# One queue for all transfers, or the stores of the weight sums on GpSimd's own

## The chip, the cores and the metric

The kernel runs on one core of a Trainium2 chip. A core has TensorE (PE in the profile), VectorE (DVE), ScalarE (ACT), GpSimd (POOL) and SyncE (SP), each with its own queue of instructions that run in order. The metric is the time of one execution in microseconds (us).

## The reference, cut to what matters

Two layers of a trunk over 1024 rows of width 1024. Layer 0 mixes with a gated MLP, layer 1 with differential attention; after each comes a ConvFFN. The large products are those of the ConvFFN, 1024 -> 5632 and 2816 -> 1024:

```python
def conv_ffn(x, w_up, conv_w, conv_b, w_down):
    h = causal_dwconv(x @ w_up, conv_w, conv_b)
    g, u = h[..., :D_FF], h[..., D_FF:]
    return (jax.nn.gelu(g) * u) @ w_down
```

with `D_FF = 2816`, and for layer 1 the product `y @ w_in` that makes the values of the attention.

## The kernel before, in words

All products run in float32 split into two fp32r parts: `split` (L168) lets ScalarE cast the high part (L170) and VectorE subtract the low part (L173), and every product is three passes of matmuls (`mm`, L160, the matmul at L162).

The products are Winograd products: a product of 2 by 2 blocks takes seven block products in place of eight, and for that needs sums of weight blocks. There are two kinds of them.

- **Up-projection weights.** `ffn` (L1142) works through 22 pairs `j` of columns. For each pair `winograd_weights` (L1029) loads two raw tiles `wr` from `in_ffn_up` by `raw_w` (L177, 512 KB each), and GpSimd makes four sums from them: L1044, L1047, L1048, L1052, always in that order on its queue. ScalarE and VectorE split the blocks and the sums (`w<-wr`, `w<-wt`) into a ring of seven `w4` tiles, which TensorE uses. ScalarE's cast of L1052's sum is its third `w<-wt` cast of a pair. The two L1153 per pair are the start of the convolution, once TensorE has made the pair's columns.
- **Down-projection and value weights.** These sums are needed only later, so `weight_sum` (L429) makes them early, one small piece at a time, and puts them aside in DRAM: it loads a piece of `in_ffn_down` (or `in_b_wv`) into a `wr` tile by two transfers (L438), lets GpSimd do four subtractions in place on 128x256 (L442 to L445), and stores the tile's two halves to `td` (or `tv`) by two transfers (L447, 256 KB each). Pairs 4 to 21 of both layers make one such sum each, pairs 8, 11, 14 and 17 two; pairs 2 and 3 of layer 0 make one for `tv`, and six more for `tv` are made in the gated MLP of layer 0. That is 52 sums and 104 stores.

The `wr` tiles of both kinds come from one ring of four buffers. In the built program the first `in_ffn_up` load of pair j+1 takes the very buffer that the sum of pair j was stored from. In a pair with two sums the second sum's load takes that buffer, and after its store the second load of pair j+1.

All transfers are begun by SP's one queue, in the order of the built program, which a scheduler fixes. A transfer that waits holds up the ones behind it.

In the gated MLP (`gmlp`), GpSimd also adds the spatial gate (L645), ScalarE copies the next gate out of PSUM (L643) into one of two buffers that L645 reads, and behind that copy on ScalarE's queue stand casts (L170) for TensorE.

Of the kernel before, what the change touches and what calls it, by code (L numbers as in the profile page):

```python
# [64 lines left out]
def trunk(ctx: ExitStack, tc: tile.TileContext, io):  # L65
    nc = tc.nc
# [7 lines left out]
    def nm(s):  # L74
        uid[0] += 1
        return f"{s}_{uid[0]}"
# [352 lines left out]
    def weight_sum(w, o, j):  # L429

        a = wpool.tile([P, 2, 2, 256], F32, tag="wr", name=nm("wr"), bufs=4)
        kt, cs = j // 2, slice(j % 2 * 256, j % 2 * 256 + 256)
        for k in range(2):
            src = w[kt + k * o.shape[1]].rearrange("p (b c) -> p b c", b=2)
            nc.sync.dma_start(a[:, k], src[:, :, cs])  # L438

        def rest():  # L440
            sub = nc.gpsimd.tensor_tensor
            sub(a[:, 0, 0], a[:, 0, 1], a[:, 0, 0], ALU.subtract)  # L442
            sub(a[:, 0, 1], a[:, 1, 1], a[:, 0, 1], ALU.subtract)
            sub(a[:, 1, 1], a[:, 1, 1], a[:, 0, 0], ALU.subtract)
            sub(a[:, 1, 0], a[:, 1, 0], a[:, 1, 1], ALU.subtract)  # L445
            for k in range(2):
                nc.sync.dma_start(o[k, kt][:, :, cs], a[:, k])  # L447

        return rest

# [892 lines left out]
```

## Time and profile before

| | us |
|---|---|
| median of 3 runs | 2171.81 (2171.61 to 2175.49) |
| the profiled execution | 2170.53 |
| its span | 2168.8 |
| TensorE busy in the span | 2113.0 (97%) |
| VectorE busy | 1660.5 (77%) |
| ScalarE busy | 1094.4 (50%) |
| GpSimd busy | 748.1 (34%) |

The profile is one execution. Its span is the time from the first to the last instruction; the profiled execution took 1.7 us more. Instructions that begin transfers do not count as busy; in a timeline they stand as SPq. The FFN of layer 0 lies at about 308 to 740 us, that of layer 1 at about 1510 to 1950 us, the gated MLP before 215 us.

### The profile page before, as it was taken

To read this page: it belongs to the slowest core of one execution; us is meant where nothing else is said; L and a number is where in the kernel's file an instruction comes from. 1 tells how busy PE (TensorE), PEld (TensorE's weight loads), DVE (VectorE), ACT (ScalarE), POOL (GpSimd) and SP (SyncE) were. 2 spreads that over 40 slices of the span, in tenths; PEclk is the share of its full clock that TensorE was granted. 3 is DMA by queue.
4 is the path that set the end of the run, shared out by engine and by line. 5 is a ranking of instruction groups with operands and counts; after the bars stand their busy time and mean duration, and the time that the engine had idled before them with its cause. 6 is when DMAs were issued, how large, how long until landed. Compare 5 with 4: busy or idle time off the path is not lost.

```text
span 2168.8 us, 27265 instructions
## 1 busy us (share of the span) xinstructions
PE 2113.0 (97%) x10008; PEld 1721.4 (79%) x10008; DVE 1660.5 (77%) x2031; ACT 1094.4 (50%) x1923; POOL 748.1 (34%) x691
## 2 busy tenths in 40 slices
PE   8989998999999999999999999999899999999998
PEld 7868776888888878887777777778688888888886
DVE  5755569878888786688588888866988888888756
ACT  7423435454545544465366665754555554454533
POOL 0463136666667000042001101222555666620012
PEclk9999999999999999999999999999999999999999
DMA  8332422544444562453411110233234444457324
GB/s 320 102 122 83 176 87 82 192 149 153 146 165 146 198 251 95 136 180 106 158 45 45 50 49 21 88 136 126 70 121 167 159 156 157 154 182 266 105 92 167
DMA packets 159270, 292.82 MB, mean 135 GB/s; under 512 B 12704, under 2 KB 77088, under 8 KB 159136
## 3 DMA queue, kind: packets, MB, share of 16 engines
q1 hardware_dynamic: 159136, 291.08, 39.3%
q8 instruction: 78, 1.28, 0.2%
q14 instruction: 56, 0.46, 0.1%
HBM read 214.49 MB, written 76.55 MB: 134 GB/s over the span
## 4 chain that ended last, share of the span: by engine, by line
PE 74%; DVE 9%; ACT 3%; issue 1%; POOL 0%; DMA 0%; DVEq 0%; ACTq 0%; POOLq 0%; SPq 0%
PE ps L162 70%; PE pst L162 2%; DVE t L173 2%; DVE w L173 1%; ACT e L885 1%; DVE t L1155 1%; PE pst L904 1%; PE pst L334 1%; DVE cols L1090 1%; DVE xs L344 0%; DVE e L891 0%; DVE h L385 0%; DVE sm L882 0%; DVE t L495 0%; ACT y L340 0%
## 5 line engine op out<-in xcount | busy, mean ns | idle before, releaser
L162 PE MATMUL ps<-t,w 128*128 128x512 f32 x4848 | 1150.8, 394 | 19.5 <-ACT tm L1086 7.8
L162 PEld LDWEIGHTS ps<-t,w 128*128 128x128 f32 x4848 | 899.2, 188 | 220.8 <-ACT tm L1086 11.6
L162 PE MATMUL ps<-w,t 128*128 128x512 f32 x2512 | 590.5, 392 | 9.0 <-ACT w L170 7.3
L162 PEld LDWEIGHTS ps<-w,t 128*128 128x128 f32 x2512 | 469.4, 188 | 107.1 <-ACT w L170 8.0
L173 DVE TENSOR_TENSOR w<-wr,w 128x512 fp32r<-128x512 f32 (+1 forms) x274 | 290.4, 1066 | 170.0 <-ACT w L170 84.3
L170 ACT CAST w<-wr 128x512 fp32r<-128x512 f32 (+1 forms) x276 | 219.1, 802 | 207.3 <-PE ps L162 195.2
L1155 DVE SCALAR_TENSOR_TENSOR t<-cols,cw,t 128x1023 f32<-128x1023 f32 (+1 forms) x176 | 264.1, 1500 | 18.9 <-ACT t L1153 16.8
L173 DVE TENSOR_TENSOR w<-wt,w 128x512 fp32r<-128x512 f32 x176 | 174.9, 1005 | 15.4 <-ACT w L170 15.2
L1086 ACT COPY tm<-ps 128x512 f32<-128x512 f32 x136 | 78.9, 580 | 146.7 <-PE ps L162 146.6
L173 DVE TENSOR_TENSOR t<-t,t 128x1024 fp32r<-128x1024 f32 (+1 forms) x124 | 134.0, 1109 | 14.4 <-ACT t L170 14.0
L170 ACT CAST t<-t 128x1024 fp32r<-128x1024 f32 (+1 forms) x124 | 105.7, 889 | 71.7 <-PE ps L162 59.4
L1153 ACT ACTIVATE t<-cols,cw 128x1024 f32<-128x1024 f32 x88 | 109.7, 1247 | 60.0 <-DVE cols L1090 59.8
L1044 POOL TENSOR_TENSOR wt<-wr,wr 128x512 f32<-128x512 f32 x44 | 67.3, 1529 | 195.5 <-DMA wr<-in_ffn_up 135.4
L162 PE MATMUL ps<-t,t 64*128 64x512 f32 (+4 forms) x792 | 128.3, 373 | 0.8 <-ACT e L885 0.4
L170 ACT CAST w<-wt 128x512 fp32r<-128x512 f32 x176 | 107.5, 622 | 23.2 <-PE ps L162 14.1
L559 POOL TENSOR_TENSOR v<-v,u 128x512 f32<-128x512 f32 x8 | 12.0, 1499 | 307.0 <-DVE u L558 307.0
L162 PEld LDWEIGHTS ps<-t,t 64*128 64x128 f32 (+1 forms) x792 | 90.3, 185 | 34.3 <-issue 11.0
L885 ACT ACTIVATE e<-ps,sm 128x128 f32<-128x128 f32 (+7 forms) x128 | 94.2, 744 | 28.8 <-DVE sm L877 22.7
L380 POOL TENSOR_SCALAR sm<-sm 128x1 f32<-128x1 f32 x32 | 22.3, 697 | 244.9 <-ACT y L378 244.6
L202 POOL TENSOR_SCALAR sm<-sm 128x1 f32<-128x1 f32 (+1 forms) x42 | 12.7, 303 | 263.7 <-ACT ot L924 161.2
L1090 DVE TENSOR_TENSOR cols<-ps,tm 128x512 f32<-128x512 f32 x132 | 90.1, 682 | 16.7 <-PE ps L162 15.0
L173 POOL TENSOR_TENSOR t<-wr,t 128x1024 fp32r<-128x1024 f32 (+1 forms) x16 | 36.4, 2282 | 167.9 <-ACT t L170 159.7
(156 smaller groups left out, 2480.4 us busy)
## 6 DMA issues: line engine op xcount, KB each, us to landing
wr<-in_ffn_up SPq DMA_DIRECT2D x88, 512.0 KB, 4.0
wr<-in_ffn_down SPq DMA_DIRECT2D x94, 256.0 KB, 3.7
pd<-t SPq DMA_DIRECT2D x88, 256.0 KB, 2.6
td<-wr SPq DMA_DIRECT2D x88, 256.0 KB, 2.5
wr<-td SPq DMA_DIRECT2D x40, 512.0 KB, 3.7
t<-pd SPq DMA_DIRECT2D x16, 1024.0 KB, 8.2
wr<-in_ffn_down SPq DMA_DIRECT2D x30, 512.0 KB, 3.6
hd<-h SPq DMA_DIRECT2D x24, 512.0 KB, 2.6
```

The costliest lines, as they stand in the source:

```text
L162: nc.tensor.matmul(o, a, b, start=first, stop=last, skip_group_check=onto)
L170: i = nc.scalar.copy(hi, src)
L173: return (engine or nc.vector).tensor_tensor(lo, src, hi.bitcast(F32), ALU.subtract)
L334: nc.tensor.transpose(pt[:, k * P:(k + 1) * P], xs[:, f:f + P], ident)
L380: nc.gpsimd.tensor_scalar(ss, sq[:, 0:1], sq[:, 1:2], EPS, ALU.add, ALU.add)
L885: nc.scalar.activation(e[:, :L], si[i], AF.Exp, bias=negm[:, i:i + 1], accum_out=sm[:, i:i + 1])
L904: nc.tensor.transpose(pt[:, k * P:(k + 1) * P], attn[:, c:c + P], ident)
L1044: i = nc.gpsimd.tensor_tensor(t1, b12, b11, ALU.subtract)
L1086: nc.scalar.copy(t, o)
L1090: nc.vector.tensor_tensor(o, a, b, ALU.add)
L1153: nc.scalar.activation(tt, src, AF.Identity, bias=c[:, 3:4], scale=c[:, 2:3])
L1155: nc.vector.scalar_tensor_tensor(tt[:, tap:], src[:, :S - tap], c[:, 2 - tap:3 - tap], tt[:, tap:], ALU.mult, ALU.add)
```

## The change

The two stores at the end of `weight_sum` are begun by GpSimd's queue. Nothing is computed differently.

```diff
             sub(a[:, 1, 1], a[:, 1, 1], a[:, 0, 0], ALU.subtract)
             sub(a[:, 1, 0], a[:, 1, 0], a[:, 1, 1], ALU.subtract)
             for k in range(2):
-                nc.sync.dma_start(o[k, kt][:, :, cs], a[:, k])
+                nc.gpsimd.dma_start(o[k, kt][:, :, cs], a[:, k])
```

The scheduler then orders the queues anew. The orders of TensorE, VectorE and ScalarE stay as they were. GpSimd's queue in pair 8 of layer 0, which makes two sums (`wr_3888` is the first sum's tile, `wr_3786` and `wr_3788` are the pair's raw weights, `wt_...` their sums):

```order
 L443 TENSOR_TENSOR wr_3888<-wr_3888 128x256
 L444 TENSOR_TENSOR wr_3888<-wr_3888 128x256
+L447 DMA td_77<-wr_3888 256x1x256
+L1048 TENSOR_TENSOR wt_3868<-wr_3786,wt_3866 128x512
 L445 TENSOR_TENSOR wr_3888<-wr_3888 128x256
-L1048 TENSOR_TENSOR wt_3868<-wr_3786,wt_3866 128x512
+L447 DMA td_77<-wr_3888 256x1x256
 L1052 TENSOR_TENSOR wt_3867<-wr_3788 128x512
```

The first store now stands on GpSimd's queue behind L444, L1048 has moved ahead of the last subtraction L445, and the second store stands behind that; this is so in pairs 5 to 21 of both layers, while in pairs 2 to 4 L1048 stays where it was relative to L445.

SP's queue in the same pair (`wr_3897` is the second sum's tile, `wr_3948` and `wr_3950` are the raw weights of pair 9):

```order
 L438 DMA wr_3888<-in_ffn_down 128x2x256 x2
-L447 DMA td_77<-wr_3888 256x1x256
 L1162 DMA pd_75<-t_3547 128x512 x2
-L447 DMA td_77<-wr_3888 256x1x256
 L438 DMA wr_3897<-in_ffn_down 128x2x256 x2
 L177 DMA wr_3948<-in_ffn_up 128x1024
-L447 DMA td_77<-wr_3897 256x1x256 x2
 L177 DMA wr_3950<-in_ffn_up 128x1024
```

The stores are gone and the loads keep their order; which buffer follows which in the ring is unchanged, so the loads that take a stored sum's buffer still wait for its stores to land.

GpSimd's queue in the gated MLP, at the third of the six `tv` sums (`wr_1551`; `wr_1632` is the fourth):

```order
 L444 TENSOR_TENSOR wr_1551<-wr_1551 128x256
+L447 DMA tv<-wr_1551 256x1x256
 L445 TENSOR_TENSOR wr_1551<-wr_1551 128x256
+L447 DMA tv<-wr_1551 256x1x256
 L645 TENSOR_TENSOR t_35_190<-t_35_190,gt_1065 128x256
+L645 TENSOR_TENSOR t_35_190<-t_35_190,gt_1074 128x256
+L645 TENSOR_TENSOR t_35_190<-t_35_190,gt_1083 128x256
 L442 TENSOR_TENSOR wr_1632<-wr_1632 128x256
-L645 TENSOR_TENSOR t_35_190<-t_35_190,gt_1074 128x256
```

Two stores come ahead of the gate additions L645, and two of these additions have moved ahead of the next sum's first subtraction.

## Rows read from the trace of the kernel before

**Rows 1.** Page, parts 1 and 3: busy us by engine; the data queue.

```profile
PE 2113.0 (97%) x10008; PEld 1721.4 (79%) x10008; DVE 1660.5 (77%) x2031; ACT 1094.4 (50%) x1923; POOL 748.1 (34%) x691
...
q1 hardware_dynamic: 159136, 291.08, 39.3%
```

**Rows 2.** Stretches of gated MLP and FFN 0: length, busy us by engine.

```profile
88.00:250.00 162.00, 151.93 (x692) 124.47 (x690) 91.10 (x127) 55.43 (x89) 69.27 (x126) 0.97 0.38 125
...
330.00:740.00 410.00, 403.79 (x1772) 331.78 (x1773) 348.40 (x337) 213.75 (x313) 250.36 (x178) 1.00 0.45 153
```

**Rows 3.** Timeline, pair 16 of layer 0: start us, length, instruction, idle before.

```profile
607.10 1.29 POOL L1044 TENSOR_TENSOR wt<-wr,wr 128x512 f32<-128x512 f32 x1 [3.46 <-DVE w L173]
...
613.29 0.74 POOL L445 TENSOR_TENSOR wr<-wr 128x256 f32<-128x256 f32 x1
...
615.58 0.57 SPq L447 DMA_DIRECT2D td<-wr  x1
...
618.55 0.81 SPq L177 DMA_DIRECT2D wr<-in_ffn_up  x2
...
623.49 1.60 POOL L1044 TENSOR_TENSOR wt<-wr,wr 128x512 f32<-128x512 f32 x1 [5.49 <-DMA wr<-in_ffn_up]
```

**Rows 4.** Timeline, pair 17 with two sums, then L1044 of pairs 18 and 20.

```profile
631.24 0.57 SPq L447 DMA_DIRECT2D td<-wr  x1
...
633.85 1.25 SPq L438 DMA_DIRECT2D wr<-in_ffn_down  x2
...
640.31 3.38 SPq L447 DMA_DIRECT2D td<-wr  x2
...
645.92 0.34 SPq L177 DMA_DIRECT2D wr<-in_ffn_up  x1
...
649.60 1.28 POOL L1044 TENSOR_TENSOR wt<-wr,wr 128x512 f32<-128x512 f32 x1 [6.50 <-DMA wr<-in_ffn_up]
...
681.63 1.34 POOL L1044 TENSOR_TENSOR wt<-wr,wr 128x512 f32<-128x512 f32 x1 [4.61 <-DMA wr<-in_ffn_up]
```

**Rows 5.** Waits of SP's queue: waiter, what released it: us, times, longest.

```profile
SPq L177 <- DMA td<-wr: 73.5, 36, 3.7
```

**Rows 6.** Timeline: L1153 of two pairs that follow each other, TensorE's pace.

```profile
652.03 1.25 ACT L1153 ACTIVATE t<-cols,cw 128x1024 f32<-128x1024 f32 x1
...
671.07 1.25 ACT L1153 ACTIVATE t<-cols,cw 128x1024 f32<-128x1024 f32 x1
```

**Rows 7.** GpSimd by shape, then VectorE: count, busy us, mean ns, idle before.

```profile
L1048 POOL TENSOR_TENSOR wt<-wr,wt 128x512 f32<-128x512 f32 x44 | 72.3, 1644 | 7.5 <-DVE w L173 7.3
...
L445 POOL TENSOR_TENSOR wr<-wr 128x256 f32<-128x256 f32 x52 | 60.0, 1155 | 3.8
...
L173 DVE TENSOR_TENSOR w<-wr,w 128x512 fp32r<-128x512 f32 (+1 forms) x274 | 290.4, 1066 | 170.0 <-ACT w L170 84.3
```

**Rows 8.** The stores: ns min/median/max to begin one; KB, us to landing.

```profile
L447 SPq DMA_DIRECT2D td<-wr x88: 560/562/569, 388.7 to 1913.1; - x88
...
td<-wr SPq DMA_DIRECT2D x88, 256.0 KB, 2.5
```

**Rows 9.** Timeline, pair 18: L1052, its cast, ScalarE's next copy.

```profile
659.10 2.28 POOL L1052 TENSOR_TENSOR wt<-wr 128x512 f32<-128x512 f32 x1
...
662.39 0.62 ACT L170 CAST w<-wt 128x512 fp32r<-128x512 f32 x1
...
664.63 0.59 ACT L1086 COPY tm<-ps 128x512 f32<-128x512 f32 x1 [1.61 <-PE ps L162]
```

**Rows 10.** Timeline, pair 21 of layer 0, then of layer 1: L1052, its cast.

```profile
707.31 1.74 POOL L1052 TENSOR_TENSOR wt<-wr 128x512 f32<-128x512 f32 x1
...
719.51 0.62 ACT L170 CAST w<-wt 128x512 fp32r<-128x512 f32 x1
...
1914.33 1.73 POOL L1052 TENSOR_TENSOR wt<-wr 128x512 f32<-128x512 f32 x1
...
1927.07 0.62 ACT L170 CAST w<-wt 128x512 fp32r<-128x512 f32 x1
```

**Rows 11.** Timeline, layer 1: L1044 of pair 3 and of pair 8.

```profile
1561.86 2.12 POOL L1044 TENSOR_TENSOR wt<-wr,wr 128x512 f32<-128x512 f32 x1 [4.38 <-DMA wr<-in_ffn_up]
...
1652.56 1.89 POOL L1044 TENSOR_TENSOR wt<-wr,wr 128x512 f32<-128x512 f32 x1 [4.39 <-DMA wr<-in_ffn_up]
```

**Rows 12.** Timeline, gated MLP: GpSimd, ScalarE and TensorE around one wait.

```profile
132.33 0.72 POOL L645 TENSOR_TENSOR t<-t,gt 128x256 f32<-128x256 f32 x1
...
133.08 0.37 ACT L643 COPY gt<-ps 128x256 f32<-128x256 f32 x1 [2.39 <-POOL t L645]
...
134.45 0.38 PE L162 MATMUL ps<-wsp,vp 128*128 128x256 f32 x1 [2.05 <-ACT vp L170]
```

## The prediction

> **What bounds the kernel now.** I read the busy shares first: TensorE is busy 2113.0 us of the span of 2168.8 [rows 1], so 55.8 us in all could be won, and any loss must come from a wait that is hidden today. The stretches come next. TensorE idles 10.1 us of 162 in the gated MLP, and 6.2 of 410 in FFN 0 [rows 2], where 88 of the 104 moved stores lie (both FFNs) and 4 more.
>
> So the question is what TensorE's work in the FFN hides. The timeline of GpSimd and SP shows a **loop** from one pair to the next [rows 3]: L1044 starts at 607.10, the sum's last store is begun at 615.58, the next raw weights' load goes out at 618.55, and the next L1044, released by that load, starts at 623.49. That is 8.5 + 3.0 + 4.9 = 16.4 us. The load waits for the store because it takes the buffer that the store reads; SP's queue stood so 36 times before an `in_ffn_up` load, 73.5 us in all [rows 5]. In a pair with two sums the loop has two stores in a row: from 623.49 over the stores at 631.24 and 640.31 and the loads at 633.85 and 645.92 to 649.60, 26.1 us [rows 3, 4]. TensorE's pace is 19.0 us a pair, from L1153 to L1153 [rows 6]. Three pairs, one of them with two sums, take the loop 681.63 - 623.49 = 58.1 us and TensorE 57.1. The loop has hardly any room on average: GpSimd lives on a lead over TensorE.
>
> How large that lead is, is read at L1052 and the ScalarE cast that takes its sum. In pair 18, after two sums, L1052 ends at 661.38 and the cast starts at 662.39, only 1.0 us later [rows 9]. In pair 21, the last, the gap is 719.51 - 709.05 = 10.5 us in layer 0 and 1927.07 - 1916.06 = 11.0 in layer 1 [rows 10]: this is what the loop may lose over a whole FFN before ScalarE waits.
>
> **The change part by part.** Removed: 104 stores from SP's queue, 0.56 us each to begin [rows 8]. SP is off TensorE's path except through the loop, where only the last store's 0.56 us counts; I take it off there and cost the other at nothing, since SP is then waiting for the landing anyway.
>
> Added: 104 stores on GpSimd's queue. No transfer of the profile is begun by GpSimd; all data go by one queue [rows 1], so their **price c** has to be bounded. Below, c = 0: GpSimd's sequencer hands it on and the engine goes on. Above, c = 2.5 us: GpSimd stands as long as such a store takes on SP from its start to its landing [rows 8]. The nearest rows are SP's 0.56 us for the very same transfer and GpSimd's own work on the very same data, one subtraction of 128x256 at 1.16 us [rows 7, 8]. I take 1.16, since it is an instruction of this engine over this tile and pays what this engine pays beside VectorE. For the landing after that I keep SP's 2.5 - 0.56 = 1.94 us.
>
> By the Trainium skill (DMA: Bandwidth & Descriptors, Specifications) the first byte comes after about 1 us on GpSimd's path and 0.6 on SP's; an estimate with c = 1.0 from that page would make the result about 2242. No run here shows it.
>
> Moved: L1048 goes ahead of the last subtraction in pairs 5 to 21, 1.64 us [rows 7], and so into the loop. Its sum comes no later, so that is all it does.
>
> The loop grows, for each pair: one sum, L1048 moved: 1.64 + 2c - 0.56 = 3.40. Two sums: 1.64 + 4c - 2 x 0.56 = 5.16. One sum, L1048 not moved (pair 4 of both layers, pairs 2 and 3 of layer 0): 2c - 0.56 = 1.76. The loop of pair 21 leads nowhere. Layer 0: 12 x 3.40 + 4 x 5.16 + 3 x 1.76 = 66.7 us. Layer 1: 12 x 3.40 + 4 x 5.16 + 1.76 = 63.2 us.
>
> What hides it: in layer 0 the 10.5 us, less 2c = 2.3, because two stores now stand ahead of L1052 too, plus what ScalarE can be late before TensorE stands. For the last term the ends are 1.6 us, ScalarE's idle time before its next copy out of PSUM [rows 9], and 9.1, its idle time in a pair (48% of 19.0, as 213.75 of 410 are busy [rows 2]); I take 5. That makes 13.2. In layer 1 it is 11.0 - 2.3 + 5 = 13.7, and 10.7 more: from pair 3 to pair 8 the loops took 90.7 us [rows 11], though five of 16.0 (the mean of pairs 18 and 19 [rows 4]) are 80.0; they waited there for buffers that TensorE's pace frees, and can take that back. That makes 24.4. When that cover is gone, TensorE runs at the loop's pace. So TensorE waits 66.7 - 13.2 = 53.5 us in layer 0 and 63.2 - 24.4 = 38.8 in layer 1, together 92.3.
>
> What gives some back: VectorE is busy 348.40 of 410 us [rows 2], and beside it a subtraction takes 1.16 us on average and can take 0.74, a sum of 512 columns 1.64 and 1.29 [rows 3, 7]. Four of the former and three of the latter in the loop lose 4 x 0.42 + 3 x 0.35 = 2.7 us to it. If the stretch grows by 46 us, VectorE's share falls from 85 to 76%, so 11% of that, 0.3 us, comes back in each of 36 loops: -11.
>
> The gated MLP: 12 stores, 13.9 us of GpSimd in a stretch where TensorE waits through ScalarE's copies for the additions L645 [rows 12]. At the wait shown two stores now stand ahead of it: up to +2.3. But two later additions now come ahead of a subtraction that waits for its load, and SP is free for that load. Ends: -10.1, all of TensorE's idle time there, and +13.9, all twelve on the path; I take +3, close to the one place that the rows show.
>
> Sum: 92.3 - 11 + 3 = +84 us. On the profiled execution that is 2170.5 + 84 = 2255; its median stands 1.3 higher, so 2256.
>
> **The rivals.**
> *Cheap stores.* For a price c the loops grow by 13.4 + 46c in layer 0 and 14.5 + 42c in layer 1, against a cover of 15.5 - 2c and 26.7 - 2c. Up to c = 0.04 both are hidden, whatever SP's queue does, and the time stays 2172; at c = 0.13 layer 0 is 4 us over (0.2%), at SP's 0.56 the sum is +34 and gives 2206. The same holds if the stores were not really carried out by GpSimd. For it: the small instructions of GpSimd are short. Against it: GpSimd's queue runs in order, and its rows of this size are not below 0.7 us. 0.11, of which 0.08 within 0.2%.
>
> *Dearer stores.* Beside a busy VectorE a GpSimd instruction already stretches from 0.74 to 1.16. If each store must also sit out a VectorE instruction of 1.07 us [rows 7], c is 2.23, the loops grow by 116 and 108 us, TensorE waits some 190, and with -20 and +7 for the other terms that gives 2350; at c = 2.5 it would be 2374. Against it: the subtractions read both their operands from the same memory as VectorE does, and a store begun need not. 0.11. The Trainium skill (SBUF — State Buffer, SBUF: two separate sides) holds against this change that a transfer begun by GpSimd waits for its descriptors while VectorE holds the ports they share, 0.62 us against 3.1 in one measurement; with 3.1 as c, an estimate from that page, the result would be about 2425. In this trace only the stretch of the subtractions bears on it.
>
> *Faster.* In the gated MLP SP's queue stands for each sum's stores, with loads behind them. If that, and not GpSimd, is what holds the additions L645 back, TensorE's 10.1 us there [rows 2] go, and the time is 2161. It decides only while c stays under 0.04, since from there on the FFN loop takes more. 0.06.
>
> **How the numbers follow.** Forecast, a loop that sets the pace of both FFNs: 0.72, at 2256. Its own spread comes from c: 2206 at 0.56, 2374 at 2.5. The range of 2185 to 2350 holds it nearly whole with half of the dearer case, and leaves out faster (0.06), most of the cheap case (0.09) and about 0.05 above. A measurement of this kernel can tell about 0.2%, 4.3 us, from no change: faster 0.06, same 0.08, slower 0.86.
>
> **What would show it.** Right: the queue of GpSimd shows L447 at about 1.2 us each; L1044 follows L1044 after some 19.5 us in pairs with one sum and 31 with two; ScalarE's casts `w<-wt` wait for GpSimd, and TensorE's idle time in the two FFN stretches rises from 6 to about 50 and 40 us, most of it behind pairs 8, 11, 14 and 17; the rest of the kernel keeps its times. Wrong: an unchanged step of L1044 (cheap stores), a step that stretches with TensorE still busy (more cover than I counted), or new waits outside the FFN.

## The result and the profile after

The changed kernel takes 2233.3 us (median of four) against 2173.65 before in the same comparison: 1.0269 times as long, with an interval of 1.0249 to 1.0289, 58 us. Three of its executions took 2230.75 to 2235.59 us; the fourth, at a granted clock of 0.56, took 3506.59 and is left out of the ratio. (All differences between kernels below are made like this one: 2173 us times what the ratio is above 1.) The forecast was 2256 us in a range of 2185 to 2350, slower: the side and the loop came out, the size of 84 us was some 45% too large.

The page of the profiled execution (2231.0 us), busy us and share of the span, then the data queues:

```profile
span 2228.8 us, 27247 instructions
...
PE 2136.1 (96%) x10008; PEld 1736.7 (78%) x10008; DVE 1693.9 (76%) x2031; ACT 1091.7 (49%) x1923; POOL 790.6 (35%) x795
...
q1 hardware_dynamic: 130848, 263.81, 34.7%
q0 software_dynamic: 8320, 27.27, 3.5%
```

Against [rows 1], TensorE's idle time rose from 55.8 to 2228.8 - 2136.1 = 92.7 us, by 37, and its busy time by 23 with the same 10008 matmuls. VectorE is busy 33 us longer too, with the same instructions. The stores' 27 MB have moved to a second queue.

Where the 37 and the 23 lie is seen in stretches of about three pairs each, layer 0 and then layer 1 (length, busy us by engine, granted clock of TensorE, DMA share, GB/s):

```profile
487.00:545.00 58.00, 58.00 (x257) 47.88 (x256) 48.54 (x45) 29.55 (x44) 38.22 (x35) 1.00 0.39 129
545.00:611.00 66.00, 62.23 (x268) 51.07 (x267) 51.38 (x45) 28.05 (x42) 40.34 (x35) 0.97 0.40 133
611.00:677.00 66.00, 59.31 (x252) 48.00 (x251) 50.80 (x45) 28.49 (x43) 40.42 (x37) 0.97 0.42 136
677.00:743.00 66.00, 61.44 (x256) 49.89 (x255) 53.07 (x47) 30.35 (x45) 40.16 (x34) 0.95 0.44 141
...
1724.00:1790.00 66.00, 66.00 (x292) 54.30 (x291) 57.53 (x52) 33.38 (x48) 40.84 (x36) 1.00 0.40 137
1790.00:1856.00 66.00, 61.27 (x260) 50.24 (x259) 49.00 (x45) 28.67 (x42) 41.46 (x38) 0.95 0.40 136
```

In the first row of each layer TensorE never stands, and runs at the full 2.4 GHz. From 545 and 1790 us on, each 66 us hold 59 to 62 us of work, where before three pairs took 57 [rows 6], and the granted clock averages 0.95 to 0.97 of 2.4 GHz, so it was at 1.2 GHz for some of the time. In the stretches shown it is below 1.00 only where TensorE paused. So part of the wait is filled with slower matmuls and counts as busy. Where the loop sets the pace, the slower matmuls need not cost time of their own; the runs do not separate the two.

The loop that answers to [rows 3], pair 16 of layer 0: GpSimd, then SP, then the L1044 of pairs 17 and 18.

```profile
637.14 1.30 POOL L1044 TENSOR_TENSOR wt<-wr,wr 128x512 f32<-128x512 f32 x1 [7.10 <-DMA wr<-in_ffn_up]
...
645.09 0.68 POOL L447 DMA_DIRECT2D td<-wr  x1
645.70 1.39 POOL L1048 TENSOR_TENSOR wt<-wr,wt 128x512 f32<-128x512 f32 x1
646.95 0.82 POOL L445 TENSOR_TENSOR wr<-wr 128x256 f32<-128x256 f32 x1
648.18 0.68 POOL L447 DMA_DIRECT2D td<-wr  x1 [0.41 <-POOL wr L445]
...
650.81 0.81 SPq L177 DMA_DIRECT2D wr<-in_ffn_up  x2
...
656.07 1.29 POOL L1044 TENSOR_TENSOR wt<-wr,wr 128x512 f32<-128x512 f32 x1 [5.88 <-DMA wr<-in_ffn_up]
...
684.72 1.26 POOL L1044 TENSOR_TENSOR wt<-wr,wr 128x512 f32<-128x512 f32 x1 [5.60 <-DVE t L1155]
```

L1044 to L1044 is 18.9 us with one sum and 28.7 with two, against 16.4 and 26.1. Two such pairs and one with two sums take 66.5 us; TensorE's work for three pairs takes 57.1. From one L1044 to the next, over the 12 pairs with one sum among pairs 5 to 20 of layer 0, the mean rose from 16.2 to 18.95, and 2.6 us of that lie ahead of the end of L445. The landing is as it was, 2.5 us from the store's start, as these rows of the stores (ns min/median/max; KB, us to landing) show beside [rows 8]:

```profile
L447 POOL DMA_DIRECT2D td<-wr x88: 666/682/776, 389.0 to 1987.8; - x88
...
td<-wr POOLq DMA_DIRECT2D x88, 256.0 KB, 2.5
```

Who waits for it is in the waits of ScalarE and TensorE (waiter, releaser: us, times, longest). Before, the first of these lines was 2.3 us and the last 7.8.

```profile
ACT w L170 <- POOL wt L1052: 83.7, 20, 6.1
...
ACT w L170 <- POOL wt L1047: 32.5, 13, 4.9
...
PE ps L162 <- ACT tm L1086: 39.6, 18, 4.7
```

### The profile page after: what moved, and what is told of

Same layout as the page of the kernel before. It is cut to its first block, busy times and chain, and to the rows that moved or that the text cites. A ratio compares the mean times of both kernels' runs of the same rounds, so it can differ in the third digit from the quotient of the medians.

```text
span 2228.8 us, 27247 instructions
## 1 busy us (share of the span) xinstructions
PE 2136.1 (96%) x10008; PEld 1736.7 (78%) x10008; DVE 1693.9 (76%) x2031; ACT 1091.7 (49%) x1923; POOL 790.6 (35%) x795
## 4 chain that ended last, share of the span: by engine, by line
PE 56%; DVE 14%; DMA 7%; POOL 5%; ACT 4%; issue 4%; SPq 0%; POOLq 0%; DVEq 0%; ACTq 0%
PE ps L162 51%; DVE t L1155 4%; DMA wr<-in_ffn_up 3%; DVE w L173 2%; PE pst L162 2%; DVE t L173 2%; DMA td<-wr 2%; PE pst L904 1%; ACT e L885 1%; ACT t L1153 1%; DVE cols L1090 1%; DMA wr<-in_ffn_down 1%; POOL wr L444 1%; POOL wt L1048 1%; POOL wt L1047 1%
## 5 line engine op out<-in xcount | busy, mean ns | idle before, releaser
L162 PE MATMUL ps<-t,w 128*128 128x512 f32 x4848 | 1170.1, 398 | 52.5 <-ACT tm L1086 39.6
L162 PEld LDWEIGHTS ps<-t,w 128*128 128x128 f32 x4848 | 910.4, 191 | 261.8 <-ACT tm L1086 48.9
L1155 DVE SCALAR_TENSOR_TENSOR t<-cols,cw,t 128x1023 f32<-128x1023 f32 (+1 forms) x176 | 287.9, 1636 | 18.0 <-ACT t L1153 16.2
L1044 POOL TENSOR_TENSOR wt<-wr,wr 128x512 f32<-128x512 f32 x44 | 68.2, 1550 | 219.6 <-DMA wr<-in_ffn_up 195.5
L1153 ACT ACTIVATE t<-cols,cw 128x1024 f32<-128x1024 f32 x88 | 109.6, 1245 | 72.3 <-DVE cols L1090 72.1
L1086 ACT COPY tm<-ps 128x512 f32<-128x512 f32 x136 | 78.8, 579 | 112.9 <-PE ps L162 112.9
L1090 DVE TENSOR_TENSOR cols<-ps,tm 128x512 f32<-128x512 f32 x132 | 90.1, 682 | 10.5 <-PE ps L162 9.7
```

Of the source, the lines that this page charges most:

```text
L162: nc.tensor.matmul(o, a, b, start=first, stop=last, skip_group_check=onto)
L1044: i = nc.gpsimd.tensor_tensor(t1, b12, b11, ALU.subtract)
L1086: nc.scalar.copy(t, o)
L1090: nc.vector.tensor_tensor(o, a, b, ALU.add)
L1153: nc.scalar.activation(tt, src, AF.Identity, bias=c[:, 3:4], scale=c[:, 2:3])
L1155: nc.vector.scalar_tensor_tensor(tt[:, tap:], src[:, :S - tap], c[:, 2 - tap:3 - tap], tt[:, tap:], ALU.mult, ALU.add)
```

## The experiments

Theory A is the loop. The rivals were that the stores cost by being on GpSimd, whatever the buffer (B), and that the moved L1048, not the stores, makes the loss. Ratios are against the kernel before on the same chip.

### Two parts of the change alone

Only the `tv` stores on GpSimd, 12 in the gated MLP and 4 in pairs 2 and 3 of layer 0:

```diff
-                nc.sync.dma_start(o[k, kt][:, :, cs], a[:, k])
+                (nc.gpsimd if w is io["b_wv"] else nc.sync).dma_start(o[k, kt][:, :, cs], a[:, k])
```

> Only the 16 stores of the value weights' sums (12 in the gated MLP, 4 in pairs 2 and 3 of layer 0) are begun by GpSimd, the 88 td stores by SP. Theory A: the two loops of pairs 2 and 3 grow by 2 x 0.68 - 0.56 = 0.8 us each and are hidden, so what is left is the gated MLP: +3 us, 2173 to 2178. Rival (the loss of the gated MLP is carried into the FFN, or the loss at pair 3 is made by the tv sums): +8 or more, 2180 upward.

Measured: 2180.3 us, 1.0032 (1.0022 to 1.0042), so 7 us. That is more than the 3 of the gated MLP, and what the rival forecast (2180 upward). In the changed kernel, which has the same rows there, the first L1044 of layer 0 starts 3.4 us late, and by the end of pair 2 TensorE is 8 us late: pairs 1 and 2, on which the forecast put nothing, add over 4 us. Which wait makes these 4 us was not followed up.

All stores on SP, only L1048 moved as the change moves it:

```diff
-        nc.gpsimd.tensor_tensor(t4, b21, t2, ALU.subtract)
+        last_t4[:] = [nc.gpsimd.tensor_tensor(t4, b21, t2, ALU.subtract)]
...
-            sub(a[:, 1, 0], a[:, 1, 0], a[:, 1, 1], ALU.subtract)
+            i = sub(a[:, 1, 0], a[:, 1, 0], a[:, 1, 1], ALU.subtract); o is not tv and tc.add_manual_dep(i.ins, last_t4[0].ins.name, mybir.DependencyInfo(mybir.DependencyClass.NoSync, mybir.DependencyReason.DATA), reason="order")
```

> All stores stay on SP; only L1048 is moved ahead of the last subtraction L445 (of the pair's first sum), in pairs 4 to 21 of both layers, as the change does in pairs 5 to 21. Theory A: each of 17 loops per layer grows by 1.64 us, 28 us per layer, against a cover of 15.5 us in layer 0 and 26.7 in layer 1: +12 and +1, so about 2185 us (2178 to 2195). Rival (the order does nothing, since GpSimd waits anyway and the whole loss comes from the stores): 2170 to 2176. Rival (no cover at all): +56, 2228.

Measured: 2207.9 us, 1.0137 (1.0121 to 1.0153): 30 us, where 13 were expected. (The medians are 35 us apart, the figure that two expectations below use; the six executions spread from 2202 to 2225 us.) The order of one instruction, with every store on SP, costs half of what the whole change costs, so neither rival held. (Its profiled execution was its longest, with a span of 2223.5 us, so only the inside of a pair is read from it.) The loop with one sum is 18.8 us, 2.6 more and not 1.64, because L1048 and its neighbours run longer: L1048 takes 1.91 us on average where it took 1.64, L445 1.35 where it took 1.16. GpSimd in pair 16:

```profile
646.51 1.60 POOL L444 TENSOR_TENSOR wr<-wr 128x256 f32<-128x256 f32 x1
648.07 1.74 POOL L1048 TENSOR_TENSOR wt<-wr,wt 128x512 f32<-128x512 f32 x1
649.77 1.72 POOL L445 TENSOR_TENSOR wr<-wr 128x256 f32<-128x256 f32 x1
651.44 1.74 POOL L1052 TENSOR_TENSOR wt<-wr 128x512 f32<-128x512 f32 x1
```

L445 took 0.74 us in that pair before [rows 3]. So a moved instruction cost its own time and changed that of its neighbours too. That they now stand beside other instructions of VectorE is the likely reason; it was not tried by itself.

The reverse, the changed kernel with L1048 put back behind the second store:

```diff
-                nc.gpsimd.dma_start(o[k, kt][:, :, cs], a[:, k])
+                i = nc.gpsimd.dma_start(o[k, kt][:, :, cs], a[:, k]); k and o is not tv and last_t4 and tc.add_manual_dep(last_t4.pop().ins, i.ins.name, mybir.DependencyInfo(mybir.DependencyClass.NoSync, mybir.DependencyReason.DATA), reason="order")
```

> The changed kernel with L1048 put back behind the sum (behind its second store), so that the loop holds the two stores but not L1048. Theory A with the run before (L1048 alone cost 35 us): the loops shrink by about 1.6 us, 26 per layer, so most of the loss goes: 2185 to 2200 us. Rival (the stores alone make the loss, L1048's place is a detail): 2215 to 2231.

Measured: 2192.9 us, 1.0096 (1.0080 to 1.0112). Of 58 us 37 go with L1048's place; the stores themselves leave 21, 7 of them the `tv` stores'. (30 alone and 21 alone do not add up to 58: the parts are not independent.) The rival that the stores alone make the loss fell.

### Cutting the loop

A first attempt gave the sums a buffer of their own, for which room was made in a small unused stretch (an added order, not shown, keeps a sum's loads behind the pair's raw loads):

```diff
-        a = wpool.tile([P, 2, 2, 256], F32, tag="wr", name=nm("wr"), bufs=4)
+        a = (own or wpool).tile([P, 2, 2, 256], F32, tag="ws" if own else "wr", name=nm("wr"), bufs=1 if own else 4)
...
-    expo = base.tile([P, 112], F32, tag="expo", name="expo")[:, :8]
+    expo = base.tile([P, 8], F32, tag="expo", name="expo")[:, :8]
```

> The stores stay on GpSimd, but in the FFNs the weight sums get one buffer of their own, so that no load of raw up-projection weights takes a buffer that a store reads; a sum's load stands behind the pair's second raw load. Theory A (the loop from L1044 over the sum's stores and their landing to the next raw weights' load sets the pace): the loop is cut, GpSimd's own work in a pair with one sum is 4 x 1.6 + 4 x 1.05 + 2 x 0.68 = 12.0 us against TensorE's 19.0, so the loss in the FFNs goes and only the gated MLP's 3 us stays: 2170 to 2182 us. Rival B (the stores cost what they cost as GpSimd's own time, or as a second stream of transfers that slows the others, wherever the buffer is): the time stays within 10 us of the changed kernel, 2223 to 2243.

> The same buffer of their own for the weight sums, with the stores on SP as in the kernel before: shows what the buffer does by itself. Both theories: 2163 to 2178 us, since TensorE idles only 6 us in FFN 0 before; if the buffer helps the kernel before as well, by no more than some 10 us.

Measured: 2241.7 us, 1.0316 (1.0302 to 1.0330), with the stores on GpSimd; 2213.0, 1.0184 (1.0170 to 1.0199), with them on SP. Both theories missed, since TensorE's pace had become 19.6 us a pair, without waits in the second kernel's FFN. The shortened tile alone, in the kernel before, shows why:

```diff
-    expo = base.tile([P, 112], F32, tag="expo", name="expo")[:, :8]
+    expo = base.tile([P, 8], F32, tag="expo", name="expo")[:, :8]
```

> The kernel before with one unused stretch of a small tile cut off (448 to 32 bytes per partition), which moves all tiles behind it by 416 bytes and changes no instruction. It tells why TensorE's pace in the runs with a buffer of their own was 19.6 us a pair without any wait, against 19.0. Theory: the shifted addresses make it: the pace is 19.6 here too, and the time 2200 to 2215 us. Rival (the busier GpSimd and SP slow TensorE, or the buffer itself): 2170 to 2176.

Measured: 2211.3 us, 1.0179 (1.0165 to 1.0193). The group of FFN matmuls on its page (busy us, mean ns, idle before) is

```profile
L162 PE MATMUL ps<-t,w 128*128 128x512 f32 x4848 | 1183.8, 400 | 17.0 <-ACT tm L1086 5.8
```

where the kernel before has 1150.8 us and 394 ns. So the 40 us of the second kernel were the shifted addresses (39 us here), and its buffer cost nothing. Between the two kernels with a buffer of their own, equal in this, 29 us remain for the stores on GpSimd, the `tv` stores among them. That was against theory A alone, and called for a cleaner cut.

The cleaner cut keeps that small tile. Only the second store reads a tile of its own, of 2 KB, so the ring's buffer comes free with the first store's landing and the last subtraction. Against the changed kernel:

```diff
-            sub = nc.gpsimd.tensor_tensor
+            sub, b = nc.gpsimd.tensor_tensor, own.tile([P, 2, 256], F32, tag="ws", name=nm("ws"), bufs=1) if own else a[:, 1]
...
-            sub(a[:, 1, 1], a[:, 1, 1], a[:, 0, 0], ALU.subtract)
-            sub(a[:, 1, 0], a[:, 1, 0], a[:, 1, 1], ALU.subtract)
+            sub(b[:, 1], a[:, 1, 1], a[:, 0, 0], ALU.subtract)
+            i = sub(b[:, 0], a[:, 1, 0], b[:, 1], ALU.subtract); last_t4 and tc.add_manual_dep(i.ins, last_t4[0].ins.name, mybir.DependencyInfo(mybir.DependencyClass.NoSync, mybir.DependencyReason.DATA), reason="order")
...
-                nc.gpsimd.dma_start(o[k, kt][:, :, cs], a[:, k])
+                nc.gpsimd.dma_start(o[k, kt][:, :, cs], b if k else a[:, 0])
```

Of the four kernels, the first is this one. The second is the one before with the same tile (without the added order), the third has the tile, the stores on SP and L1048 ahead of L445, the fourth the tile and the stores on GpSimd without the added order.

> The changed kernel, but in the FFNs the last two subtractions of a sum write to a 2 KB tile of their own, and the second store reads that tile; so the buffer that the next raw weights' load takes comes free with the first store's landing and the last subtraction, not with the second store's landing. Both stores stay on GpSimd, L1048 stays ahead of L445, and the orders of the other engines are those of the changed kernel. Theory A (the loop through the stored buffer): a pair with one sum loses the 0.4 us before the second store and its 2.5 us to landing, 18.9 - 2.9 = 16.0 us, as in the kernel before; the loss in the FFNs goes: 2172 to 2185 us. Rival B (the stores cost by GpSimd's own time, or by a second stream of transfers): no more than a few us go, 2220 to 2235.

> The same tile of its own for the second store, in the kernel before (stores on SP). Theory A: loops shorter by some 3 us under an FFN that idles only about 6 and 2 us: a gain of 0 to 8 us, 2164 to 2173. Rival: no change, or a loss through an order of SP's queue that has moved: 2172 to 2185.

> All stores on SP, the second store from a tile of its own, and L1048 ahead of L445: in the FFNs GpSimd's own work is in the order of e5_half_own, only its stores are gone. Theory (L1048's place cost 35 us in e4_l1048_moved only through the loop over the stored buffer; what remains in e5_half_own is the stores on GpSimd beside VectorE, 16 us, and the tv stores, 7): 2172 to 2180 us. Rival (L1048's place costs by itself): 2190 to 2208.

> As the run e5_half_own (stores on GpSimd, the second store from a tile of its own), but L1048 is not pinned ahead of L445: it stands between L445 and the second store. Since the loop is already cut, the theory that the rest of the loss (2198 against 2180 with the tv stores alone) is made by the stores beside VectorE says: no more than 5 us change, 2192 to 2203. Rival (the rest is still the loop, through L1048): 2178 to 2186.

| stores on | tile of its own | L1048 | us | ratio and interval |
|---|---|---|---|---|
| SP | no | behind L445 | 2172 to 2174 | 1 |
| SP | no | ahead of L445 | 2207.9 | 1.0137 (1.0121 to 1.0153) |
| GpSimd | no | ahead of L445 | 2233.3 | 1.0269 (1.0249 to 1.0289) |
| GpSimd | no | behind the second store | 2192.9 | 1.0096 (1.0080 to 1.0112) |
| SP | yes | behind L445 | 2174.8 | 1.0005 (0.9996 to 1.0014) |
| SP | yes | ahead of L445 | 2178.0 | 1.0023 (1.0009 to 1.0036) |
| GpSimd | yes | ahead of L445 | 2198.2 | 1.0122 (1.0102 to 1.0141) |
| GpSimd | yes | between L445 and the second store | 2204.4 | 1.0145 (1.0121 to 1.0169) |

Two things follow. L1048's place cost 30 us with the shared buffer and 4 with the tile: it cost through the loop and hardly otherwise. And cutting the loop takes 32 of the changed kernel's 58 us away, after which ScalarE waits for L1052 nowhere in the FFNs; but 26 stay, of which the same work with the stores on SP shows 5. So theory A explains more than half, and some 21 us belong to the stores being on GpSimd, 7 of them to the `tv` stores. Theory A's own forecast for this run, up to 2185, was missed by 13, and rival B's, from 2220 on, by 22. That the second queue slows the other transfers does not show: the loads of `in_ffn_up` land in 4.4 us here and in 4.5 with the stores on SP. (In the changed kernel they stay at 4.0; the stores `pd<-t`, still on SP, land there in 4.7 us instead of 2.6, and the loads of `in_ffn_down` in 4.4 instead of 3.7.)

Of the other three, the tile alone brought no gain (its rival's forecast), and with the tile, the stores on SP and L1048 ahead of L445 the time was as forecast. The last came out 1 us above its range and some 6 us slower than the first: VectorE is busy 1745.5 us in it, against 1711.0 in the first, and 37 of its instructions take over 2.45 us, against 17. With L1048 behind the second store the changed kernel loses less, shared buffer and all, than either kernel with the tile and the stores on GpSimd, so what stands right behind a store on GpSimd's queue matters beside the loop. No version beat the kernel before.

### What a begun transfer costs by itself

To the kernel with the stores on SP and the loop cut (2178.0 us), two transfers per sum in the FFNs were added on GpSimd, of a constant tile to an unused place. The FFNs make 46 sums, so these are 92 transfers; the expectations' "92 sums" and "92 x 2" are a miscount.

```diff
+            i = sub(b[:, 1], a[:, 1, 1], a[:, 0, 0], ALU.subtract); own and tc.add_manual_dep(nc.gpsimd.dma_start(ds[dn.pop(), :, :, :64], ident.rearrange("p (b c) -> p b c", b=2)).ins, i.ins.name, mybir.DependencyInfo(mybir.DependencyClass.NoSync, mybir.DependencyReason.DATA), reason="order")
```

(the same behind L445; the second kernel moves `ident[:1, :64]` only.)

> As the run e10_half_own_sp_l1048 (all stores on SP, the loop cut, 2178 us), and GpSimd begins, behind L444 and behind L445 of each of the 92 sums in the FFNs, one transfer of a constant tile to an unused place in DRAM: 256 pieces as a store has, but 64 KB, and nothing waits for it. It measures the begun transfer by itself, without the loop and without the sums' data. Theory (what remained in e5_half_own is GpSimd's begun transfers beside VectorE): 2190 to 2205 us, and VectorE's instructions that read two operands from SBUF and start beside such a transfer take above 1.6 us on average, up to 3. Rival (what remained came from the landing of the sums' data in a second queue, or from the order): 2174 to 2184.

> The same 92 x 2 added transfers, but of 256 bytes in 16 pieces each. Theory (GpSimd's time for a begun transfer, and with it VectorE's wait, goes with the pieces that it writes): below 0.4 us each on GpSimd, 2176 to 2186 us. Rival (a begun transfer has one price, whatever it moves): 0.68 us each, and the time of e11_unrelated_stores within 5 us.

Measured: 2205.5 us, 1.0157 (1.0144 to 1.0170), and 2202.1, 1.0163 (1.0134 to 1.0193). Nothing waits for these transfers, and yet they cost 29 and 30 us beyond the 5 of the kernel that they were added to (by the medians 28 and 24). The first time is half a microsecond above its forecast. The first kernel shows how. GpSimd, then VectorE, at one place:

```profile
562.27 0.67 POOL L444 DMA_DIRECT2D ds<-ident  x1
562.88 1.37 POOL L1048 TENSOR_TENSOR wt<-wr,wt 128x512 f32<-128x512 f32 x1
564.13 0.82 POOL L445 TENSOR_TENSOR ws<-wr,ws 128x256 f32<-128x256 f32 x1
564.82 0.77 POOL L445 DMA_DIRECT2D ds<-ident  x1
565.43 1.47 POOL L1052 TENSOR_TENSOR wt<-wr 128x512 f32<-128x512 f32 x1
...
562.53 4.94 DVE L173 TENSOR_TENSOR w<-wt,w 128x512 fp32r<-128x512 f32 x1 [0.81 <-ACT w L170]
567.39 0.68 DVE L1090 TENSOR_TENSOR cols<-ps,tm 128x512 f32<-128x512 f32 x1
```

VectorE's subtraction starts while GpSimd begins a transfer, and ends at 567.47, 0.6 us after the last of four further GpSimd instructions: it seems to have got nothing done until GpSimd paused, for the like instruction just before it took 0.68 us. GpSimd's own instructions run fast meanwhile, L445 in 0.82 us. In the kernel before no instruction of VectorE took over 2.41 us, and in the kernel without the added transfers one took over 2.45; here 34 did, the longest 5.09. Of those that read two operands from SBUF, 18 start while a transfer is being begun, and they take 3.5 us on average, more than was forecast. Instructions that read one operand from PSUM are not touched. The groups of VectorE in the kernel without the added transfers, then with them:

```profile
L173 DVE TENSOR_TENSOR w<-wr,w 128x512 fp32r<-128x512 f32 (+1 forms) x274 | 281.6, 1034 | 171.9 <-ACT w L170 86.9 <-PE ps L162 66.8 <-issue 14.9
...
L1090 DVE TENSOR_TENSOR cols<-ps,tm 128x512 f32<-128x512 f32 x132 | 90.3, 684 | 24.2 <-PE ps L162 22.7 <-ACT tm L1086 1.4
```

```profile
L173 DVE TENSOR_TENSOR w<-wr,w 128x512 fp32r<-128x512 f32 (+1 forms) x274 | 342.3, 1262 | 126.4 <-PE ps L162 67.2 <-ACT w L170 41.1 <-issue 14.9
...
L1090 DVE TENSOR_TENSOR cols<-ps,tm 128x512 f32<-128x512 f32 x132 | 90.0, 682 | 15.8 <-PE ps L162 14.2 <-ACT tm L1086 1.4
```

How this reaches TensorE shows at another place of the same kernel:

```profile
1724.28 0.66 POOL L444 DMA_DIRECT2D ds<-ident  x1
...
1724.47 5.01 DVE L173 TENSOR_TENSOR w<-wr,w 128x512 fp32r<-128x512 f32 x1 [1.44 <-ACT w L170]
...
1730.60 0.68 DVE L1090 TENSOR_TENSOR cols<-ps,tm 128x512 f32<-128x512 f32 x1
...
1731.32 1.24 ACT L1153 ACTIVATE t<-cols,cw 128x1024 f32<-128x1024 f32 x1 [4.64 <-DVE cols L1090]
...
1733.53 0.57 ACT L1086 COPY tm<-ps 128x512 f32<-128x512 f32 x1
...
1734.15 2.32 PE L162 MATMUL ps<-t,w 128*128 128x512 f32 x7 [2.69 <-ACT tm L1086]
```

The late subtraction makes VectorE's L1090 late, ScalarE's L1153 waits for that, the copy L1086 stands behind L1153 on ScalarE's queue, and TensorE waits for the copy. Nine of TensorE's ten waits of over 0.5 us in the middle of the two FFNs (380 to 790 and 1590 to 2010 us) follow a VectorE instruction of 4.4 to 5.1 us in this way, 2.1 to 2.7 us each. In the kernel with the cut loop and the stores on GpSimd nine of ten such waits do too, behind VectorE instructions of 2.7 to 3.1 us beside a store or the instructions next to it.

In the changed kernel the long VectorE instruction stands at 579.42: VectorE's L1160 takes 3.27 us beside a store, L1048 and L445.

```profile
578.89 0.69 POOL L447 DMA_DIRECT2D td<-wr  x1
579.51 1.40 POOL L1048 TENSOR_TENSOR wt<-wr,wt 128x512 f32<-128x512 f32 x1
580.75 0.84 POOL L445 TENSOR_TENSOR wr<-wr 128x256 f32<-128x256 f32 x1
...
579.42 3.27 DVE L1160 TENSOR_TENSOR t<-t,t 128x1024 f32<-128x1024 f32 x1
```

By the Trainium skill (SBUF — State Buffer, Who interferes with whom) the ports that VectorE and GpSimd share are a lock, held for a whole instruction by whichever of a VectorE instruction with two SBUF inputs and a GpSimd instruction that reads SBUF starts first. The rows agree that VectorE stands while GpSimd works (4.94 us), and that an instruction with a PSUM operand (0.68 us) is spared; they show more than one GpSimd instruction passing before VectorE gets its turn.

The small transfer was to tell whether the price goes with the pieces moved. It mostly does not. GpSimd's time for it, in the second kernel:

```profile
L444 POOL DMA_DIRECT2D ds<-ident x46 | 24.4, 530 | 0.0
L445 POOL DMA_DIRECT2D ds<-ident x46 | 24.1, 523 | 0.0
```

256 bytes cost 0.53 us, 64 KB in 256 pieces 0.67 to 0.74, a store of 256 KB 0.68. The forecast of under 0.4 us and 2186 at most fell; the rival's time held, its price of 0.68 us did not. Part of the loss is of the same make: eight of TensorE's twelve waits in the same stretches follow a VectorE instruction of 3.0 to 4.4 us beside the second transfer. But VectorE is busy only 1687.0 us there, against 1743.1 with the larger transfers and 1652.0 without any, and the loads of `in_ffn_up` land in 5.4 us instead of 4.5; TensorE's longest wait, 5.1 us, stands behind a cast that waited 4.3 us for such a load. Why they land later, and how much of the loss that is, stays open.

## Why the prediction was right, and where its sizes were off

**What bounds the kernel, and the loop** were right. The wait named (ScalarE's casts `w<-wt` for GpSimd) is the one that appeared, and TensorE then waits for ScalarE's `tm`. About two thirds of TensorE's idle time in the FFNs from pair 5 on stands right behind pairs 11, 14 and 17; none stands behind pair 8, where the lead was not yet used up. Cutting the buffer's round trip removes 32 of 58 us.

**The price c** was the step that failed: 1.16 us taken, 0.68 measured. The row chosen was GpSimd's subtraction of the same tile, on the ground that the store would pay beside VectorE as that does. It does not: 666 to 776 ns over 88 `td` stores, and 881 at most over the 16 `tv` stores. SP's 0.56 us, the other near row, was the better neighbour. With 0.68 the prediction's own formulas give growths of 13.4 + 46 x 0.68 = 44.7 and 14.5 + 42 x 0.68 = 43.1 us, covers of 14.1 and 25.3, and so 30.6 + 17.8 = 48.4 us. Measured from the L1153 of pair 5 to that of pair 21, layer 0 and layer 1 of the changed kernel,

```profile
449.77 1.25 ACT L1153 ACTIVATE t<-cols,cw 128x1024 f32<-128x1024 f32 x1
...
776.92 1.25 ACT L1153 ACTIVATE t<-cols,cw 128x1024 f32<-128x1024 f32 x1
...
1685.96 1.25 ACT L1153 ACTIVATE t<-cols,cw 128x1024 f32<-128x1024 f32 x1
...
2009.84 1.25 ACT L1153 ACTIVATE t<-cols,cw 128x1024 f32<-128x1024 f32 x1
```

they take 327.2 and 323.9 us, against 300.0 and 301.0 before (442.41 to 742.38 and 1648.94 to 1949.94): 27.2 + 22.9 = 50.1 us. With that price the prediction's whole sum would be 48.4 - 6 + 3 = +45 us, some 2217 (an estimate from its own formulas, with the relief scaled to the growth): the price made the forecast some 39 us too large, and smaller terms that were wrong the other way hid 13 of these.

**The steps of the loop**: forecast 19.5 and 31 us, measured 18.9 and 28.7, again the price. **The landing** was right: 2.5 us from the store's start on either queue, although the 0.41 us between L445 and the second store was not seen. The Trainium skill (DMA: Bandwidth & Descriptors, Specifications) gives GpSimd's path a first byte some 0.4 us later than SP's; no such difference shows here, and the c = 1.0 behind the estimate of 2242 was too high as well.

**L1048** was put into the loop at the right places and with 1.64 us, but as one term among several. "So that is all it does" was wrong: alone it cost 30 us where the same reckoning gives 13, since it and its neighbours stretched too. That the 50 us fit the formulas all the same is partly luck: behind a store GpSimd's instructions run fast, L1052 in 1.49 us on average instead of 1.81, so the changed kernel's loop gets that back.

**The relief of 11 us** pointed the wrong way. GpSimd did win time from VectorE, but not because VectorE's share fell: it shuts VectorE out behind a store, and VectorE is busy 33 us more. Once the loop is cut, the stores on GpSimd cost about 21 us, 7 of them the `tv` stores'; how much of that the loop hides in the changed kernel is not shown.

**The cover** held roughly. Paced loops of layer 1 were to be taken back, and were in part: from pair 3 to pair 8 (1598.94 to 1691.65 us) the five loops take 92.7 us against 90.7 [rows 11], 2.0 more, where 0.8 + 3 x 2.44 = 8.1 would be due with c = 0.68. From pair 5 to pair 21 the loops grew by 45.0 us in layer 0 (L1044 at 398.49 and 741.91, before 399.24 and 697.66) and by 36.1 in layer 1 (1634.52 and 1975.98, before 1596.85 and 1902.25), and TensorE by 27.2 and 22.9. So 17.8 us were hidden in layer 0, and 13.2 and the 6.1 taken back in layer 1, for 14.1 and 25.3 by the formulas.

**The gated MLP**: +3 forecast, 3.4 measured up to the first L1044 of layer 0. The 4 us of pairs 1 and 2 were missed. With the 50.1 us of the FFNs these make up the 58.

**TensorE's waits**: about 50 and 40 us were to show as idle time in the FFNs. The rise is 37 us in the whole kernel; the slower matmuls fill part of the rest, and counting idle time alone would have made the loss look smaller than it is.

**The rivals.** Cheap stores (2206 at SP's price) came close to being the case: c is nearer to 0.56 than to 1.16, and the time is still 27 us higher. Dearer stores fell: no store took over 0.88 us, while VectorE was at work beside most of them. It was the other engine that waited. The trap that the Trainium skill (SBUF — State Buffer, SBUF: two separate sides) tells of needs a VectorE instruction in a mode that takes both of the shared ports, as a copy of float32 does. VectorE ran no copy beside the stores, so these runs do not test it. Faster through the gated MLP fell.

## What to carry to other kernels

Before moving a transfer to another queue, follow the buffer it reads: if a load waits for its landing, every microsecond ahead of the store on its new queue is in a loop, and where that loop has no room to spare it decides, not the busy share. Look at what the scheduler moves along with it: here one reordered subtraction cost more than the stores did. And a transfer begun by GpSimd is not paid by GpSimd alone: VectorE instructions with both operands in SBUF can wait beside it, so its place on GpSimd's queue matters as its count does.

## What was not expected of the hardware

- A VectorE instruction with two SBUF operands that starts beside a transfer begun by GpSimd can wait for that and for the GpSimd instructions right behind it: 18 of them took 3.5 us on average, up to 5.1. The transfer need move only 256 bytes to cost GpSimd 0.53 us.
- Moving all later tiles by 416 bytes per partition, with no instruction changed, took TensorE's pace in the FFN from 19.0 to 19.6 us a pair and the kernel from 2174 to 2211 us (1.0179, 1.0165 to 1.0193). By which rule addresses matter was not tried.
- TensorE's granted clock was 1.00 while it worked without a pause and 0.95 to 0.97 in the stretches where it paused for 4 to 7 us in 66.
